# Eighty of 128 expert blocks of U: transposed by VectorE ahead of time and read back from DRAM

## The chip, the cores and the metric

The program runs on one core of a Trainium2 chip. The metric is the device time of one execution in microseconds (us), taken as the median of three executions; lower is better. A separate execution was recorded by the hardware profiler, and every duration in this document is from such a recording.

## The reference, cut to what matters

Two blocks act on 256 tokens of 2048 float32 features. The first is a gated convolution mixer with an MLP (matrices `w_in`, `w_out`, `w_up`, `w_down`). The second is attention (`w_in_2`, `w_uq_2`, `w_ukv_2`, `w_a_proj_2`, `w_b_proj_2`, `w_o_2`) and then an expert layer:

```
q = (h @ w_q)                      # w_peer_q_2
s = q . keys                       # 8 heads, two halves, 128 keys each
expert, gate = best 16 of 16x16 sums per head, softmax   # 128 experts per token
a = einsum('cd,ced->ce', x, u[expert])        # u: 16384 x 2048
w = gelu(a) * gate
y = einsum('ce,ced->cd', w, v[expert])
```

The kernel does not gather 128 rows of u for each token over all 2048 columns. It multiplies the tokens with all 16384 rows of u over columns 640 to 2047, and picks from that product; only columns 0 to 639 are gathered.

## The kernel before, in words

Every matrix product is done in three passes of float32r matmuls: each float32 operand is split into a high part (`hi`, `uh`, written by ScalarE) and the rest (`lo`, `ul`, written by VectorE); TensorE then does hi*hi, hi*lo and lo*hi. `split` (L208, L210) is that pair.

**Dense layers.** `linear` (L268) walks over groups of 512 output columns; for each it walks over chunks of four 128-row blocks of the weight. `load_chunk` loads a chunk of 1 MB with one DMA on SP's queue into `raw` (three buffers), splits it in two halves (`hi` and `lo`, four buffers each) and 24 matmuls of 512 columns follow. After each chunk `bg.pump(pump)` issues queued background work. `post_norm` is the same for `w_out` and `w_down`, with two column groups at once and a normalisation at the end, which writes the next layer's transposed operand `xh`, `xl` through `put_xT`. The last 11 of the operand's 16 row blocks live in `xbh`, `xbl`. In order of time: `w_in`, `w_out`, `w_up`, `w_down`, front of `w_in_2`, `w_uq_2`, `w_ukv_2`, gates of `w_in_2`, projections, `w_o_2`, `w_peer_q_2`.

**U stage** (L1184 to L1230). The 16384 rows are 128 blocks of 128. For a block, one DMA on SP's queue brings 128 x 1408 numbers (704 KB) into `uraw`, two buffers. TensorE transposes it in 11 pieces of 128 x 128 (L1203, issued early by a raised priority), ScalarE and VectorE split the pieces out of PSUM in three units (4, 4 and 3 pieces; `uh`, `ul`, four buffers), and 33 matmuls of 256 columns (L1213 to L1215) form the block's product with all tokens. After a pair of blocks ScalarE copies the result to `L`. Background items (the routing: top 16 and so on, mostly VectorE) are pumped once per unit. Once they are used up, each block is followed by two or three gathered dot products: an indirect DMA from GpSimd's queue (`gt`, 320 KB) and one VectorE instruction (L1174).

**V stage.** The same in the other direction, not touched by the change.

Each engine runs its own queue in order; the order in the queues is the order of the program, modified by a planner that works with expected durations. A tile pool that is closed gives its memory to pools opened later, and their first writes wait for the last use of what lay there.

Of the kernel before, what the change touches and what calls it, by code (L numbers as in the profile page):

```python
# [12 lines left out]
F32 = mybir.dt.float32  # L13
# [7 lines left out]
P = 128  # L21
T = 256
# [10 lines left out]
DU = D - GU  # L33
DN = D - GV


# [16 lines left out]
def tile_conv_mlp_then_attention_peer(ctx, tc, a, out):  # L53
    nc = tc.nc
    PSUM = bass.MemoryType.PSUM

    cp = ctx.enter_context(tc.tile_pool(name="cp", bufs=1))
    sm = ctx.enter_context(tc.tile_pool(name="sm", bufs=3))
# [179 lines left out]
    bg = Background()  # L238

    def load_natural(w):  # L240
# [27 lines left out]
    def linear(load, xs, groups, evac, chunks, pair=1, pump=0, prep=None, skew=False, first=None):  # L268
        last = len(chunks) - 1
        for g0 in range(0, len(groups), pair):  # L270
# [17 lines left out]
            for ci, (k0, nk) in enumerate(chunks):  # L288
                if prep is not None:
                    prep(k0, nk)  # L290
                for g in gs:
# [4 lines left out]
                    else:  # L296
                        for h in range(0, nk, 2):
                            for tt in range(NT):
                                o = accs[g][tt][:, :groups[g][1]]
                                for n in (h, h + 1):  # L300
# [6 lines left out]
                                    nc.tensor.matmul(o, lhsT=xl_, rhs=hi, start=False, stop=s1)  # L307
                    bg.pump(pump)
            for tt in range(NT):
                for ci, g, parts in tail:  # L310
                    mm(ci, g, parts, tt)
                for g in gs:
                    evac(g, tt, accs[g][tt][:, :groups[g][1]])
# [14 lines left out]

    def post_norm(w, xs, gain_ap, chunks, pool, next_gain, prep=None):
        og = pool.tile([P, NT, D // 2], F32, name="og")  # L330
# [4 lines left out]
        def evac(g, tt, acc):  # L335
# [9 lines left out]
            nc.vector.tensor_tensor(scaled[tt, g], acc, gbs[g], ALU.mult)  # L345
            if g == 3:
                ssq = sm.tile([P, 1], F32, name="pn_ssq", tag="ssq")
                nc.vector.tensor_reduce(ssq, sq[tt], AX.X, ALU.add)
                y, _ = rms_scale(ssq, D, f"pn{tt}")
                for c in range(4):  # L350
                    cs = slice(c * W, (c + 1) * W)
                    nc.vector.scalar_tensor_tensor(
                        res[:, tt, cs], scaled[tt, c], y, res[:, tt, cs], ALU.mult, ALU.add
                    )
                    put_xT(tt, list(range(4 * c, 4 * c + 4)), next_gain)
# [65 lines left out]
    with ExitStack() as pa:  # L421
# [139 lines left out]

        with tc.tile_pool(name="pn", bufs=1) as pn:
            post_norm(
                a["w_out"][0], resident(yh, yl), a["mix_post_gain"][0],
                [(0, 4), (8, 4), (12, 4), (4, 4)], pn, "mlp_pre",
            )


    with ExitStack() as pb:
# [3 lines left out]
        with ExitStack() as pup:  # L573
            ev = pup.enter_context(tc.tile_pool(name="ev", bufs=2))
            _, rsq = residual_scales("n1")

            def evac_up(g, tt, acc):
# [9 lines left out]
                chunks_of(KD),  # L587
            )
        with tc.tile_pool(name="pn", bufs=1) as pn:
            zs = {}  # L590

            def prep(k0, nk):
# [6 lines left out]
            def zget(k, tt):  # L599
# [5 lines left out]
                a["w_down"][0], zget, a["mlp_post_gain"][0], chunks_of(DFF // P), pn, "g_mix",  # L605
                prep=prep,
            )


    dr = ctx.enter_context(tc.tile_pool(name="dr", bufs=1, space=bass.MemoryType.DRAM))  # L610
    NEG = -1e30
    BIG = 1e33
    with ExitStack() as pc:
# [4 lines left out]
        with ExitStack() as pat:  # L618
            at = pat.enter_context(tc.tile_pool(name="at", bufs=1))
            xp = pat.enter_context(tc.tile_pool(name="xp", bufs=1))  # L620
            ev = pat.enter_context(tc.tile_pool(name="ev", bufs=2))
            r2, _ = residual_scales("n2", last_xT["g_mix"])
            r2q = []
# [275 lines left out]
            def weave(chains):  # L899
# [10 lines left out]
                [(0, 2)], pump=2,  # L910
            )
            left_ = [swa(*s_) for s_ in spots[4:]]
            late_ = [mla(*s_) for s_ in spots]
# [5 lines left out]
            )  # L919
            bg.flush()  # L920

        with ExitStack() as pj:
            mp = pj.enter_context(tc.tile_pool(name="mx", bufs=1))
            ev = pj.enter_context(tc.tile_pool(name="ev", bufs=2))
# [35 lines left out]
            def evac_o(g, tt, acc):  # L960
# [9 lines left out]
                evac_o, chunks_of(KD), skew=True,  # L970
            )


# [34 lines left out]
    for tt in range(NT):  # L1008
        nc.vector.tensor_tensor(xg[:, tt, :], res[:, tt, 0:GU], gfb, ALU.mult)
        rd = dr.tile([P, D], F32, name=f"res_d{tt}")  # L1010
        nc.scalar.dma_start(rd, res[:, tt, :])
        res_d.append(rd)
    kraw = qp.tile([P, 16, P], F32, name="kraw")
    nc.scalar.dma_start(kraw, a["peer_keys_2"][0].rearrange("h p n d -> n (h p) d"))
# [121 lines left out]
    def load_wq(raw, k0, nk, n0, nw):  # L1136
# [11 lines left out]
        chunks_of(KD), pump=2,  # L1148
    )
    q_ctx.close()  # L1150
    st_ctx.close()
# [37 lines left out]
    for i in range(NE):  # L1189
# [6 lines left out]
        raw = us.tile([P, DU], F32, name="uraw", tag="uraw")  # L1196
        nc.sync.dma_start(raw, a["peer_u_2"][0, i * P:(i + 1) * P, GU:D])
        rawp = raw.rearrange("p (j k) -> p k j", k=KU)
        for k0, nk in UNITS:
            with tc.high_priority(offset=EARLY):  # L1200
                ut = pst.tile([P, 4, P], F32, name="tp_u", tag="tr")
                for kk in range(nk):
                    nc.tensor.transpose(ut[:, kk, :], rawp[:, k0 + kk, :], ident)  # L1203
# [249 lines left out]
```

## Time and profile before

| | us |
|---|---|
| median of three executions | 3265.41 (3259.81 to 3267.61) |
| the profiled execution's own time | 3268.55 |
| span of its trace, first to last instruction | 3266.8 |
| PE (TensorE) busy | 3148.7 (96%) |
| DVE (VectorE) busy | 2213.1 (68%) |
| ACT (ScalarE) busy | 1585.8 (49%) |
| POOL (GpSimd) busy | 852.9 (26%) |
| moved by DMA | 687.06 MB, mean 210 GB/s |

PE and PEld are matmuls and the loads of their stationary operand, which overlap. An engine's busy time counts no waits. The share of the DMA engines is the mean over the core's 16. A mean over the whole span mixes stages with different limits, so the rows below are by stage.

### The profile page before, as it was taken

The numbers are of one execution on the slowest core, as the hardware profiler recorded it, in microseconds if no ns is written. First come the engines' busy times: TensorE is split into PE (matmuls) and PEld (weight loads), VectorE is DVE, ScalarE is ACT, GpSimd is POOL, SyncE is SP. The second block draws the span as 40 slices with busy tenths as digits, with TensorE's granted clock in tenths as the row PEclk, the third lists the DMA queues.
The fourth block names the chain that finished last, engine by engine and source line by source line (L and its number), as shares of the span: only waits on it lengthen the run. The fifth ranks groups of instructions, "written<-read, shape, count | busy, mean of one in ns | idle before, by whom it ended". The sixth has DMA issues, their size and how long they took to land.

```text
span 3266.8 us, 47283 instructions
## 1 busy us (share of the span) xinstructions
PE 3148.7 (96%) x16970; PEld 2659.9 (81%) x16970; DVE 2213.1 (68%) x4331; ACT 1585.8 (49%) x2602; POOL 852.9 (26%) x793
## 2 busy tenths in 40 slices
PE   9899999999999999999999999999999999989998
PEld 7678788887888787777878999999999976667776
DVE  6987644445555655455658877766666977778887
ACT  7555544444454556455454333333333564545554
POOL 1630000000000000000002245544443965555554
PEclk9999999999999999999999999999999999999999
DMA  6445566565555454456664379878886358888887
GB/s 209 131 166 194 165 179 183 178 182 189 193 200 193 143 190 140 161 170 206 207 229 135 125 236 308 308 258 258 258 262 207 125 168 293 278 277 290 288 294 239
DMA packets 284389, 687.06 MB, mean 210 GB/s; under 512 B 23575, under 2 KB 28666, under 8 KB 283898
## 3 DMA queue, kind: packets, MB, share of 16 engines
q1 hardware_dynamic: 234864, 518.58, 47.4%
q0 software_dynamic: 40960, 151.03, 15.1%
q10 hardware_dynamic: 8330, 14.44, 1.3%
q8 instruction: 133, 2.18, 0.3%
q14 instruction: 102, 0.84, 0.1%
HBM read 675.43 MB, written 8.52 MB: 209 GB/s over the span
## 4 chain that ended last, share of the span: by engine, by line
PE 69%; DMA 14%; DVE 9%; issue 4%; POOL 1%; ACT 1%; DVEq 0%; SPq 0%; ACTq 0%; POOLq 0%
PE acc L307 15%; PE acc L306 15%; PE acc L305 15%; DMA gt<-peer_v,e 11%; PE tp_u L1203 5%; PE aps L1215 4%; PE aps L1213 4%; PE aps L1214 4%; DMA uraw<-peer_u 2%; DVE gc L446 2%; DVE lo L210 2%; DVE y L1351 1%; PE ep L1283 1%; PE wp L1314 1%; DVE vl L210 1%
## 5 line engine op out<-in xcount | busy, mean ns | idle before, releaser
L210 DVE TENSOR_TENSOR lo<-raw,hi 128x1024 fp32r<-128x1024 f32 (+2 forms) x580 | 711.7, 1229 | 536.1 <-ACT hi L208 535.5
L208 ACT ACTIVATE hi<-raw 128x1024 fp32r<-128x1024 f32 (+2 forms) x580 | 607.6, 1049 | 584.2 <-PE acc L307 553.4
L1213 PE MATMUL aps<-xbh,uh 128*128 128x256 f32 x1408 | 429.9, 305 | 0.0
L1215 PE MATMUL aps<-xbh,ul 128*128 128x256 f32 x1408 | 425.3, 302 | 0.1
L306 PE MATMUL acc<-lo,xbh 128*128 128x512 f32 (+1 forms) x1034 | 412.9, 400 | 11.8 <-DVE lo L210 11.7
L1214 PE MATMUL aps<-xbl,uh 128*128 128x256 f32 x1408 | 421.5, 299 | 0.0
L307 PE MATMUL acc<-hi,xbl 128*128 128x512 f32 (+1 forms) x1034 | 411.7, 399 | 2.4 <-DVE xbl L212 2.4
L208 ACT ACTIVATE uh<-tp_u 128x512 fp32r<-128x512 f32 (+1 forms) x384 | 215.7, 562 | 398.5 <-PE aps L1214 198.7
L305 PE MATMUL acc<-hi,xbh 128*128 128x512 f32 (+1 forms) x1034 | 408.5, 399 | 0.1
L210 DVE TENSOR_TENSOR ul<-tp_u,uh 128x512 fp32r<-128x512 f32 (+1 forms) x384 | 246.9, 643 | 207.1 <-ACT uh L208 143.3
L1167 POOL DMA_INDIRECT gt<-peer_v,e x256 | 308.2, 1204 | 286.5 <-DVE y L1351 255.4
L208 ACT ACTIVATE vh<-vraw 128x512 fp32r<-128x512 f32 x384 | 239.9, 633 | 284.1 <-DMA vraw<-peer_v 224.4
L1167 POOL DMA_INDIRECT gt<-peer_u,e x256 | 278.0, 1086 | 315.3 <-DVE gt L1174 270.8
L1402 PE MATMUL va<-vl,wh 128*128 128x512 f32 x768 | 315.5, 411 | 41.7 <-DVE vl L210 40.1
L1203 PE MATMUL tp_u<-ident,uraw 128*128 128x128 f32 x1408 | 318.8, 292 | 6.3 <-DMA uraw<-peer_u 4.5
L1403 PE MATMUL va<-vh,wl 128*128 128x512 f32 x768 | 302.2, 394 | 0.0
L1397 PE MATMUL va<-vh,wh 128*128 128x512 f32 x768 | 298.2, 393 | 2.1 <-ACT vh L208 2.0
L1213 PEld LDWEIGHTS aps<-xbh,uh 128*128 128x128 f32 x1408 | 274.8, 195 | 0.0
L1215 PEld LDWEIGHTS aps<-xbh,ul 128*128 128x128 f32 x1408 | 273.8, 194 | 0.3 <-DVE ul L210 0.3
L1214 PEld LDWEIGHTS aps<-xbl,uh 128*128 128x128 f32 x1408 | 273.6, 194 | 0.0
L1351 DVE SCALAR_TENSOR_TENSOR y<-gt,wtok,y 128x512 f32<-128x512 f32 x256 | 191.8, 749 | 113.6 <-DMA gt<-peer_v,e 111.0
L210 DVE TENSOR_TENSOR vl<-vraw,vh 128x512 fp32r<-128x512 f32 x384 | 255.8, 685 | 4.6 <-ACT vh L208 4.6
(534 smaller groups left out, 5974.3 us busy)
## 6 DMA issues: line engine op xcount, KB each, us to landing
vraw<-peer_v SPq DMA_DIRECT2D x384, 256.0 KB
raw<-w_in SPq DMA_DIRECT2D x88, 1024.0 KB
uraw<-peer_u SPq DMA_DIRECT2D x128, 704.0 KB
raw<-w_up SPq DMA_DIRECT2D x64, 1024.0 KB
raw<-w_down SPq DMA_DIRECT2D x64, 1024.0 KB
raw<-w_out SPq DMA_DIRECT2D x16, 1024.0 KB
raw<-w_o SPq DMA_DIRECT2D x16, 1024.0 KB
jb<-jd SPq DMA_DIRECT2D x32, 512.0 KB
```

The source lines that it names most:

```text
L208: op = nc.scalar.activation(hi, src, AF.Copy, scale=scale)
L210: nc.vector.tensor_tensor(lo, src, hi, ALU.subtract)
L305: nc.tensor.matmul(o, lhsT=xh_, rhs=hi, start=s0, stop=False)
L306: nc.tensor.matmul(o, lhsT=xh_, rhs=lo, start=False, stop=False)
L307: nc.tensor.matmul(o, lhsT=xl_, rhs=hi, start=False, stop=s1)
L1167: nc.gpsimd.indirect_dma_start(out=gt, out_offset=None, in_=table, in_offset=bass.IndirectOffsetOnAxis(ap=e4[:, tt, s:s + 1], axis=0),)
L1203: nc.tensor.transpose(ut[:, kk, :], rawp[:, k0 + kk, :], ident)
L1213: nc.tensor.matmul(o, lhsT=uh[:, kk, :], rhs=xbh[:, k, :], start=s0, stop=False)
L1214: nc.tensor.matmul(o, lhsT=uh[:, kk, :], rhs=xbl[:, k, :], start=False, stop=False)
L1215: nc.tensor.matmul(o, lhsT=ul[:, kk, :], rhs=xbh[:, k, :], start=False, stop=s1)
L1402: nc.tensor.matmul(acc[tt][n], lhsT=wh[:, e % 2, tk], rhs=vl, start=False, stop=False)
L1403: nc.tensor.matmul(acc[tt][n], lhsT=wl[:, e % 2, tk], rhs=vh, start=False, stop=s1)
```

## The change

A `Transposer` works on blocks i with i % 8 in (0, 1, 2, 4, 6), 80 of 128, in 160 half blocks of 64 rows. It is pumped after each chunk in `w_out`, `w_up`, `w_down`, the gates, the projections, `w_o` and `w_peer_q`, and at a rate of 0.73 it does one half block at 73 of 100 pumps. One step loads a half block by four DMAs on SP's queue (each 32 partitions by two runs of 352 numbers), transposes the half block loaded one step before with one VectorE instruction of 128 x 704 numbers, and stores that to a DRAM tile `ud` by a DMA from GpSimd's queue. The buffers `tq` and `tu` (two each) lie in pools opened next to the dense layers, and during `w_down` in the memory of `xbh`; there `xbh` is allocated anew near the end (`free_stage`). In the U stage an early block is read back in transposed order, in the same 704 KB, and split straight from `uraw`; its TensorE transposes are left out.

```diff
+QU = DU // 4
+    class Transposer:
+        def __init__(self, blocks):
+            self.todo = [(i, h) for i in blocks for h in range(2)]
+            self.done = {
+                i: dr.tile([P, 2, KU, 64], F32, name=f"ud{i}") for i in blocks
+            }
...
+        def place(self):
+            if self.pool is not None:
+                return (
+                    self.pool.tile([P, 2 * QU], F32, name="tq", tag="tq"),
+                    self.pool.tile([P, 2 * QU], F32, name="tu", tag="tu"),
+                )
+            self.turn = 1 - self.turn
+            o = 4 * QU * self.turn
+            return self.slots[:, o:o + 2 * QU], self.slots[:, o + 2 * QU:o + 4 * QU]
+
+        def pump(self):
+            if self.pool is None and self.slots is None:
+                return
+            self.credit += self.rate
+            if self.credit < 1:
+                return
+            self.credit -= 1
+            before, self.loaded = self.loaded, None
+            if self.todo:
+                i, h = self.todo.pop(0)
+                tq, tu = self.place()
+                for g in range(4):
+                    r, c = i * P + h * 64, GU + g * QU
+                    nc.sync.dma_start(
+                        tq[g * 32:(g + 1) * 32, :].rearrange("p (q c) -> p q c", q=2),
+                        a["peer_u_2"][0, r:r + 64, c:c + QU].rearrange("(q e) c -> e q c", e=32),
+                    )
+                self.loaded = i, h, tq, tu
+            self.finish(before)
+
+        def finish(self, unit):
+            if unit is None:
+                return
+            i, h, tq, tu = unit
+            nc.vector.transpose(
+                tu.rearrange("p (k q e) -> p q k e", q=2, e=32),
+                tq.rearrange("p (q c k) -> p q k c", q=2, k=KU),
+            )
+            nc.gpsimd.dma_start(
+                self.done[i][:, h].rearrange("p k e -> p (k e)"), tu
+            )
+
+        def close(self):
+            self.finish(self.loaded)
+            self.pool = self.slots = self.loaded = None
+
+    pre = Transposer([i for i in range(128) if i % 8 in (0, 1, 2, 4, 6)])
...
                     bg.pump(pump)
+                    pre.pump()
...
             if g == 3:
+                if tt == 0 and before is not None:
+                    before()
...
+            pre.open(0.73, slots=xb_pool.tile([P, 8 * QU], F32, name="stage", tag="xbh"))
+            def free_stage():
+                pre.close()
+                xh.rest = xb_pool.tile([P, KU, T], F32R, name="xbh2", tag="xbh")
...
+            px.close()
+            pre.open(0.73, px.enter_context(tc.tile_pool(name="tp", bufs=2)))
...
         raw = us.tile([P, DU], F32, name="uraw", tag="uraw")
-        nc.sync.dma_start(raw, a["peer_u_2"][0, i * P:(i + 1) * P, GU:D])
-        rawp = raw.rearrange("p (j k) -> p k j", k=KU)
+        early = i in pre.done
+        if early:
+            nc.sync.dma_start(raw, pre.done[i].rearrange("p h k e -> p (h k e)"))
+            rawt = raw.rearrange("p (h k e) -> p k h e", h=2, e=64)
+        else:
+            nc.sync.dma_start(raw, a["peer_u_2"][0, i * P:(i + 1) * P, GU:D])
+            rawp = raw.rearrange("p (j k) -> p k j", k=KU)
         for k0, nk in UNITS:
...
-            split(uh[:, :nk], ul[:, :nk], ut[:, :nk])
+            if early:
+                half = lambda t: t[:, :nk].rearrange("p k (h e) -> p k h e", h=2)
+                split(half(uh), half(ul), rawt[:, k0:k0 + nk])
+            else:
+                with tc.high_priority(offset=EARLY):
+                    ut = pst.tile([P, 4, P], F32, name="tp_u", tag="tr")
+                    for kk in range(nk):
+                        nc.tensor.transpose(ut[:, kk, :], rawp[:, k0 + kk, :], ident)
+                split(uh[:, :nk], ul[:, :nk], ut[:, :nk])
```

## Rows read from the trace of the kernel before

**Rows 1.** Page: busy us by engine; chain that ended last, by engine.

```profile
PE 3148.7 (96%) x16970; PEld 2659.9 (81%) x16970; DVE 2213.1 (68%) x4331; ACT 1585.8 (49%) x2602; POOL 852.9 (26%) x793
PE 69%; DMA 14%; DVE 9%; issue 4%; POOL 1%; ACT 1%; DVEq 0%; SPq 0%; ACTq 0%; POOLq 0%
```

**Rows 2.** Stretches: busy us per engine (instructions), PEclk, DMA share, GB/s.

```profile
365.00:745.00 380.00, 376.72 (x1672) 302.98 (x1671) 193.85 (x235) 187.84 (x249) 0.00 (x0) 0.99 0.58 174
745.00:1105.00 360.00, 357.40 (x1567) 293.15 (x1567) 205.56 (x198) 174.56 (x204) 1.50 (x2) 1.00 0.58 195
1250.00:1490.00 240.00, 236.81 (x1124) 180.37 (x1123) 125.39 (x243) 128.24 (x282) 0.00 (x0) 1.00 0.49 161
1490.00:1675.00 185.00, 185.00 (x832) 151.38 (x831) 107.59 (x117) 92.20 (x114) 0.33 (x2) 1.00 0.63 208
1675.00:1800.00 125.00, 120.40 (x566) 98.34 (x564) 98.19 (x337) 64.43 (x110) 17.35 (x19) 0.97 0.52 176
1800.00:1905.00 105.00, 104.46 (x844) 104.14 (x845) 93.96 (x335) 41.64 (x89) 24.16 (x34) 0.98 0.39 133
1905.00:2130.00 225.00, 220.95 (x1792) 218.49 (x1791) 164.80 (x361) 81.66 (x143) 125.58 (x119) 1.00 0.89 301
2130.00:2500.00 370.00, 367.91 (x3011) 367.72 (x3010) 227.44 (x478) 132.05 (x237) 148.39 (x134) 1.00 0.78 251
```

**Rows 3.** PE's timeline in one U block: start us, us, instruction.

```profile
2258.12 0.29 PE L1203 MATMUL tp_u<-ident,uraw 128*128 128x128 f32 x1
2258.62 0.30 PE L1203 MATMUL tp_u<-ident,uraw 128*128 128x128 f32 x1
2259.00 0.28 PE L1214 MATMUL aps<-xbl,uh 128*128 128x256 f32 x1
2260.19 0.29 PE L1215 MATMUL aps<-xbh,ul 128*128 128x256 f32 x1
```

**Rows 4.** Instruction groups by shape: count, busy us, mean ns, idle before.

```profile
L1203 PE MATMUL tp_u<-ident,uraw 128*128 128x128 f32 x1408 | 318.8, 292 | 6.3 <-DMA uraw<-peer_u 4.5 <-DVE gt L1174 1.4 <-DVE ul L210 0.2
L210 DVE TENSOR_TENSOR ul<-tp_u,uh 128x512 fp32r<-128x512 f32 x256 | 175.8, 687 | 95.9 <-ACT uh L208 52.2 <-PE aps L1215 34.1 <-issue 8.3
L210 DVE TENSOR_TENSOR vl<-vraw,vh 128x512 fp32r<-128x512 f32 x384 | 255.8, 685 | 4.6 <-ACT vh L208 4.6
L210 DVE TENSOR_TENSOR lo<-raw,hi 128x768 fp32r<-128x768 f32 x8 | 7.7, 957 | 10.7 <-ACT hi L208 10.7
L210 DVE TENSOR_TENSOR wl<-L,wh 128x512 fp32r<-128x512 f32 x63 | 67.8, 1076 | 1.2 <-ACT wh L208 1.2
L1275 DVE TENSOR_SCALAR jb<-jb,iota_p 128x1024 f32<-128x1024 f32 x32 | 24.8, 786 | 3.4 <-DMA jb<-jd 3.3
```

**Rows 5.** SP's and ACT's timelines: a w_up chunk issued, then first used.

```profile
503.40 0.37 SPq L242 DMA_DIRECT2D raw<-w_up  x1
...
515.40 1.06 ACT L208 ACTIVATE hi<-raw 128x1024 fp32r<-128x1024 f32 x1 [1.75 <-PE acc L307]
```

**Rows 6.** Stretches, while that chunk's DMA lands and just after.

```profile
504.40:508.60 4.20, 4.20 (x24) 3.50 (x23) 1.72 (x2) 2.14 (x3) 0.00 (x0) 1.00 0.83 250
508.60:509.30 0.70, 0.70 (x4) 0.57 (x3) 0.70 (x1) 0.00 (x0) 0.00 (x0) 1.00 0.00 0
```

**Rows 7.** SP queue's waits in w_up: us, times, longest us.

```profile
SPq L242 <- DVE lo L210: 316.7, 59, 5.8
```

**Rows 8.** Chain of waits, 1905 to 2130 us: by line, one piece.

```profile
by line: DMA uraw<-peer_u 27.4%; PE tp_u L1203 17.2%; PE aps L1215 13.5%; PE aps L1213 13.3%; PE aps L1214 13.1%; issue 12.1%; DVE gt L1174 1.7%; DVE ul L210 1.4%; ACT uh L208 0.8%; SPq L1197 0.5%; DVEq L210 0.0%; ACTq L208 0.0%
1955.15 6.94 DMA uraw<-peer_u
```

**Rows 9.** SP issuing U rows: ns min/median/max, first, last start.

```profile
L1197 SPq DMA_DIRECT2D uraw<-peer_u x128: 327/328/641, 1687.6 to 2483.9; - x128
```

**Rows 10.** Stretches: ten microseconds of dense DMA in the V stage.

```profile
2730.00:2740.00 10.00, 7.73 (x32) 5.48 (x31) 5.51 (x9) 3.61 (x6) 1.84 (x2) 1.00 0.97 359
```

More of the change, by code (lines that the diff above doesn't have):

```diff
@@ L55, in tile_conv_mlp_then_attention_peer @@
     PSUM = bass.MemoryType.PSUM
+    dr = ctx.enter_context(tc.tile_pool(name="dr", bufs=1, space=bass.MemoryType.DRAM))
     cp = ctx.enter_context(tc.tile_pool(name="cp", bufs=1))
@@ L238, in tile_conv_mlp_then_attention_peer, with open @@
     bg = Background()
+    class Transposer:
[5 more added lines that the diff above has]
+            self.pool = self.slots = self.loaded = None
+            self.credit = self.turn = 0
+        def open(self, rate, pool=None, slots=None):
+            self.rate, self.pool, self.slots = rate, pool, slots
+        def place(self):
[39 more added lines that the diff above has]
+            self.finish(self.loaded)
+            self.pool = self.slots = self.loaded = None
+    pre = Transposer([i for i in range(128) if i % 8 in (0, 1, 2, 4, 6)])
     def load_natural(w):
@@ L327, in transposed, with post_norm @@
         return tp
-    def post_norm(w, xs, gain_ap, chunks, pool, next_gain, prep=None):
+    def post_norm(w, xs, gain_ap, chunks, pool, next_gain, prep=None, before=None):
         og = pool.tile([P, NT, D // 2], F32, name="og")
@@ L560, in tile_conv_mlp_then_attention_peer @@
             bg.flush()
-        with tc.tile_pool(name="pn", bufs=1) as pn:
+        with tc.tile_pool(name="pn", bufs=1) as pn, tc.tile_pool(name="tp", bufs=2) as tpool:
+            pre.open(0.73, tpool)
             post_norm(
@@ L574, in tile_conv_mlp_then_attention_peer @@
             ev = pup.enter_context(tc.tile_pool(name="ev", bufs=2))
+            tpool = pup.enter_context(tc.tile_pool(name="tp", bufs=2))
             _, rsq = residual_scales("n1")
+            pre.open(0.73, tpool)
             def evac_up(g, tt, acc):
@@ L588, in tile_conv_mlp_then_attention_peer @@
             )
+            pre.close()
         with tc.tile_pool(name="pn", bufs=1) as pn:
             zs = {}
+            pre.open(0.73, slots=xb_pool.tile([P, 8 * QU], F32, name="stage", tag="xbh"))
+            def free_stage():
+                pre.close()
+                xh.rest = xb_pool.tile([P, KU, T], F32R, name="xbh2", tag="xbh")
             def prep(k0, nk):
@@ L605, in tile_conv_mlp_then_attention_peer @@
                 a["w_down"][0], zget, a["mlp_post_gain"][0], chunks_of(DFF // P), pn, "g_mix",
-                prep=prep,
+                prep=prep, before=free_stage,
             )
-    dr = ctx.enter_context(tc.tile_pool(name="dr", bufs=1, space=bass.MemoryType.DRAM))
+            xbh = xh.rest
     NEG = -1e30
@@ L619, in tile_conv_mlp_then_attention_peer @@
             at = pat.enter_context(tc.tile_pool(name="at", bufs=1))
-            xp = pat.enter_context(tc.tile_pool(name="xp", bufs=1))
             ev = pat.enter_context(tc.tile_pool(name="ev", bufs=2))
+            px = pat.enter_context(ExitStack())
+            xp = px.enter_context(tc.tile_pool(name="xp", bufs=1))
             r2, _ = residual_scales("n2", last_xT["g_mix"])
@@ L920, in tile_conv_mlp_then_attention_peer @@
             bg.flush()
+            pre.close()
         with ExitStack() as pj:
+            pre.open(0.73, pj.enter_context(tc.tile_pool(name="tp", bufs=2)))
             mp = pj.enter_context(tc.tile_pool(name="mx", bufs=1))
@@ L971, in tile_conv_mlp_then_attention_peer @@
             )
+            pre.close()
     NE = 128
@@ L1012, in tile_conv_mlp_then_attention_peer @@
         res_d.append(rd)
+    pre.open(0.73, q_ctx.enter_context(tc.tile_pool(name="tp", bufs=2)))
     kraw = qp.tile([P, 16, P], F32, name="kraw")
@@ L1149, in tile_conv_mlp_then_attention_peer @@
     )
+    pre.close()
+    assert not pre.todo, len(pre.todo)
     q_ctx.close()
@@ L1196, in tile_conv_mlp_then_attention_peer @@
         raw = us.tile([P, DU], F32, name="uraw", tag="uraw")
-        nc.sync.dma_start(raw, a["peer_u_2"][0, i * P:(i + 1) * P, GU:D])
-        rawp = raw.rearrange("p (j k) -> p k j", k=KU)
+        early = i in pre.done
[5 more added lines that the diff above has]
+            rawp = raw.rearrange("p (j k) -> p k j", k=KU)
         for k0, nk in UNITS:
[L1200 to L1203, printed above, removed]
             pool = ring("u")
```

## The prediction

> **What bounds the kernel now.** I read the page first: TensorE is busy for 96% of the span and makes up 69% of the chain that ended last; VectorE is busy for 68% [rows 1]. These are means, so the second view is busy time by stretch [rows 2]. In the dense layers (365 to 1675 us) PE is busy for 98 to 100% of each stretch, VectorE for 51 to 58%, the DMA engines for 49 to 63%: PE sets the pace, and the rest has room. The U stage runs from 1800 to 2500 us and has three parts. In A (1800 to 1905) VectorE is almost as full as PE, 94 of 105 us, since routing is worked off there, and DMA is at 0.39. In B (1905 to 2130) three gathers go with each block: DMA is at 0.89, and the chain of waits in that stretch names the DMA of U rows for 27.4%, with pieces of nearly 7 us [rows 8]. In C (2130 to 2500) there are two gathers per block, DMA is at 0.78, PE at 99%. At 44 PE instructions a block, the counts of rows 2 give 19, 41 and 68 blocks.
>
> **What the change takes off TensorE.** In the timeline of one block [rows 3] a transpose and a matmul alternate between 2258.12 and 2258.62: two pairs in 0.50 us, 0.25 us a pair. From 2259.00 to 2260.19 ten matmuls alone take 1.19 us, 0.119 each. So a transpose costs PE 0.131 us of its time (its shown duration of 292 ns [rows 4] overlaps its neighbours). 80 blocks x 11 = 880 of them go: 115 us of PE. By part, with five of eight blocks early: A 12 x 11 x 0.131 = 17 us, B 25.6 blocks, 37 us, C 42.5 blocks, 61 us.
>
> **What is late next in U.** The DMA brings the same bytes as before, and VectorE's split costs the same from SBUF as from PSUM (685 against 687 ns [rows 4]). So each part gets PE's new time, or what else is in it, if that is longer; as a filled engine I take a share of 0.97, the densest ten microseconds of DMA that I found [rows 10].
> - A: PE 105 - 17 = 88; VectorE 94 / 0.97 = 97. Result 97, a gain of 8.
> - B: PE 225 - 37 = 188; DMA 225 x 0.89 / 0.97 = 206. Result 207, a gain of 18.
> - C: PE 370 - 61 = 309; DMA 370 x 0.78 / 0.97 = 298. The two are within 4%, so neither hides the other's hitches; I take 320, a gain of 50.
>
> Sum 76 us, of the 115 that PE gives up. The bounds are 33 (third rival) and 115 (second).
>
> **VectorE's transposes.** No row shows one. A half block is 128 x 704 numbers. From above: the strided read of L, 128 x 512 in 1076 ns, gives 704 / 512 x 1076 = 1.48 us; from below: a one-operand instruction, 128 x 1024 in 786 ns, gives 0.54; the contiguous split in between, 128 x 768 in 957 ns, gives 0.88 [rows 4]. The transpose reads with a stride, so I take 1.48. 160 of them are 237 us (86 to 237). At 0.73 of 64 pumps, 47 lie in `w_up`: VectorE goes from 194 to 263 of 380 us; in `w_down` from 206 to 275 of 360; in projections and `w_o` (23 of them) from 108 to 142 of 185 [rows 2]. PE's work covers that, for the split runs ahead of PE: ScalarE waits 1.75 us for PE to free `hi` [rows 5]. The cover is thin only in `w_peer_q`: 98 us of 125 plus 12 x 1.48 = 17 makes 92%. I charge 7 there (0 to 17).
>
> **The transfers.** A step moves 0.36 MB in and 0.36 MB out, 115 MB in all. `w_up` moves 174 GB/s at a share of 0.58, so 300 GB/s when full: 2.4 us a step, 113 us, and the share goes from 0.58 to 0.88; in the same way `w_down` goes to 0.86 and projections with `w_o` to 0.90 [rows 2]. B has run at 0.89, so this fits, without much room. The stores wait on GpSimd's queue, which is idle from `w_up` to `w_o` (0 to 1.5 us busy [rows 2]); in `w_peer_q` they stand among its routing items, inside the 7.
>
> **The new wait on SP's queue.** The load of step n goes into the buffer that the transpose of step n-2 has to read first; that transpose stands in VectorE's queue one pump earlier, behind a chunk's splits. SP works in order, so the load of the next weight chunk stands behind this wait, where it used to wait only for `lo` of the chunk three before (316.7 us of such waits in `w_up` [rows 7]: SP is far ahead). A chunk issued at 503.40 had landed by 508.60 and was first used at 515.40 [rows 5, 6]: 6.8 us of slack. A chunk of `w_up` is 26 PE instructions at 380 / 1672 us, 5.9 us, and in `w_down` 24 at 360 / 1567, 5.5 us [rows 2]. Now a load is issued up to a chunk (5.9 us) and a transpose (1.5) later, behind four issues of 0.33 [rows 9] and the step's data (about 1.1): 9.8 us, 3 more than the slack. That lands in the second reserve, the two chunks that `hi` and `lo` hold (11.8 us less half a chunk and 2.3 of splitting, 1.06 on ScalarE and by size 1.28 on VectorE [rows 4, 5]: 6.5 us). The round from split to transpose, load, weight load and split is 1.5 + 1.3 + 1.1 + 5.2 + 3.4 (twice 1.06, once 1.28) = 12.5 us. In eight chunks the chain goes through three rounds and one plain step of 2.5 (27 of 100 pumps do nothing): 40 us, against 8 x 5.5 = 44 at PE's pace. Hidden, then, but the first rival starts here.
>
> The Trainium skill has a rule against these loads ("SBUF — State Buffer", section "Door 1: The DMA port swizzle"): a transfer's rate hangs on how many of 16 ports its partitions reach, and partitions 0 to 31 reach eight, 189 GB/s at 1 MiB. Each of the four loads of a step spans 32 partitions; an estimate by that page is 0.36 MB / 189 GB/s = 1.9 us a step in place of 1.1, a round of 13.3 us, still under PE's pace, and no other sum. No row of this trace shows a large load to 32 partitions.
>
> **Edges.** At each of six openings the first load needs memory whose last user has just finished, and SP's queue holds weight loads behind it. Slack of 6.8 us covers most; I charge 2 us each, 12 (0 to 41). At the end of `w_down` one transpose (1.48) and its store come before `xbh` is written again, behind the norm's small instructions: 2 (0 to 5).
>
> **The sum.** -76 + 7 + 12 + 2 = -55 us. The profiled execution took 3268.55 us, 1.75 over its span; it becomes 3213. It stands 3.1 above the median of the runs, so the forecast is 3210 us.
>
> **Rivals.**
> 1. *Weight loads come late (slower).* Place: SP's queue in the dense layers. The reserve is used up when the round exceeds (44 - 2.5) / 3 = 13.8 us. For it: the round is 12.5 by quiet transfers, and the DMA share nears 0.9. Against: the planner may let weight loads pass a load whose buffer isn't free. At a round of 15.5 us, eight chunks take 49 us: 0.6 us more each over 144 chunks at 5.5 (90 us), 0.2 over the 64 of `w_up` (14): +104 - 55, 3314 us.
> 2. *U follows PE alone.* DMA gives way beyond 0.97 and the gathers fill the gaps: -115 + 21, 3171 us. For it: ten microseconds at 359 GB/s [rows 10] against 301 in B. Against: the chain in B already names the DMA [rows 8].
> 3. *U rows are held too long.* In an early block `uraw` is free only when VectorE's third `ul` is done, behind dot products; before, PE's early transposes freed it. With two buffers and loads of nearly 7 us [rows 8], B gains nothing and C half: -8 - 25 + 21, 3253 us.
>
> **Chances and range.** Forecast 0.52, rival 1 0.18, rival 2 0.17, rival 3 0.13. A difference under 0.3% (10 us) can't be told from none. Forecast, rival 2 and half of rival 3 are faster (0.76), the other half is the same (0.06), rival 1 is slower (0.18). The range is 3160, below rival 2 with its edges cheaper, to 3272, past rival 3; rival 1 is what is left out.
>
> **What would show it.** Right: 528 transposes of `tp_u` are left; PE's pace in early blocks is 33 x 0.119 = 3.9 us; A, B and C take about 97, 207 and 320 us; VectorE's transposes take 0.9 to 1.5 us; the dense stretches keep PE at 97% or more, with a DMA share near 0.87. Wrong: PE waiting for `lo` or `hi` after a late `raw` between 365 and 1675 us (rival 1); a B as long as before (rival 3); a C near 309 and B under 200 (rival 2); a transpose of VectorE far above 1.5 us, which would fill `w_down` and make the splits late without any DMA.

## The result: slower, and the profile after

The changed kernel takes 3320.9 us (median of 4 runs, 3314.7 to 3323.4), the kernel before 3263.9 beside it: ratio 1.0172, interval 1.0152 to 1.0192. The forecast was 3210 us with a range to 3272, so it had the wrong sign. The profiled execution took 3314.74 us, 1.7 over its span. Page of the kernel after, against [rows 1]:

```profile
span 3313.0 us, 47230 instructions
...
PE 3070.0 (93%) x16090; PEld 2558.9 (77%) x16090; DVE 2416.2 (73%) x4491; ACT 1574.1 (48%) x2602; POOL 951.1 (29%) x953
...
PE 38%; DMA 29%; DVE 15%; issue 13%; POOL 3%; SPq 1%; ACT 1%; DVEq 0%; ACTq 0%; POOLq 0%
```

TensorE lost its 880 transposes and is busy for 79 us less, yet the span grew by 46: its share of the last chain fell from 69 to 38%, and DMA's doubled. Where this happened is read by cutting each trace at the first load of each stage (and U at its first matmul, its first gathered dot product and the 117th). One execution each, us (`w_down` with the small projections behind it, `attn` from `w_uq` to the gates; the runs under the first two are explained below):

```
              w_in  w_out   w_up  w_down  attn   proj+w_o  w_peer_q     A      B      C   pick+V, tail
before       264.9   85.8  386.2   472.9  275.2    183.0     135.6   107.9  213.0  375.3     766.9
after        284.1  138.6  384.9   494.6  273.5    197.6     125.6   123.0  200.9  319.7     770.6
dense_alone  285.4  138.0  386.3   493.3  274.6    197.4     138.2   108.4  214.7  371.3     766.5
u_alone      265.7   85.8  385.0   472.7  276.1    183.1     129.1   113.2  207.0  314.8     777.4
pinned       266.3   89.0  424.5   501.7  277.3    194.8     127.5   120.9  204.9  322.9     775.5
lag1_two     266.2   85.8  386.3   476.2  274.3    185.2     130.4   121.2  207.3  319.7     780.7
done_by_wo   266.1   89.3  385.1   478.8  270.0    195.7     126.2   113.8  197.6  320.5     771.1
late_only    265.5   85.8  385.3   479.0  269.2    189.4     128.8   103.9  205.5  315.2     770.5
```

In B and C the changed kernel won 12 and 56 us, about what was forecast (18 and 50). The dense layers took +19, +53, +22 and +15 us (`w_in`, `w_out`, `w_down`, projections with `w_o`), `w_peer_q` -10 and A +15. Stretches of the kernel after (columns as in [rows 2]): `w_in`, `w_out`, `w_up`, `w_down`, projections with `w_o`, then A, B, C:

```profile
10.00:295.00 285.00, 236.43 (x947) 180.00 (x945) 266.27 (x350) 145.68 (x235) 107.71 (x131) 0.95 0.80 257
295.00:433.00 138.00, 109.01 (x453) 87.36 (x454) 96.56 (x111) 56.77 (x65) 9.22 (x17) 0.89 0.70 223
433.00:818.00 385.00, 380.87 (x1699) 306.24 (x1698) 196.42 (x238) 190.00 (x251) 0.00 (x0) 1.00 0.58 175
818.00:1233.00 415.00, 397.11 (x1694) 320.01 (x1693) 289.56 (x315) 193.79 (x258) 27.78 (x52) 0.98 0.79 256
1587.00:1785.00 198.00, 191.30 (x851) 155.39 (x850) 140.56 (x145) 91.48 (x121) 12.46 (x23) 0.98 0.91 290
...
1908.00:2031.00 123.00, 102.49 (x800) 100.31 (x799) 110.19 (x380) 48.38 (x100) 34.56 (x40) 0.92 0.41 137
2031.00:2231.00 200.00, 178.73 (x1407) 172.35 (x1407) 153.23 (x340) 69.02 (x132) 127.48 (x115) 0.99 0.92 325
2231.00:2548.00 317.00, 308.94 (x2530) 305.44 (x2528) 230.95 (x486) 131.45 (x235) 151.72 (x132) 1.00 0.86 293
```

`w_up` is untouched: DMA share 0.58 and no work on POOL, as before. Its 47 steps, and those of `w_out`, were moved ahead of it by the planner, into `w_in` and `w_out` (39 and 19 transposes lie there). The same stages of the kernel before (`w_in`, `w_out`) show what they fell on: in `w_in` VectorE was already at 237 of 265 us (it works the convolution), in `w_out` PE never paused.

```profile
10.00:275.00 265.00, 242.71 (x1017) 190.47 (x1017) 236.97 (x356) 161.47 (x254) 90.67 (x90) 0.97 0.50 166
275.00:361.00 86.00, 86.00 (x381) 70.53 (x380) 48.27 (x48) 40.16 (x46) 0.00 (x0) 1.00 0.62 208
```

At that border SP's queue (start us, us, instructions) is filled with the new loads: 25 in a row, then three weight chunks and none until 354.79.

```profile
283.96 0.38 SPq L306 DMA_DIRECT2D raw<-w_out  x1
284.39 22.84 SPq L279 DMA_DIRECT2D tq<-peer_u  x25
317.52 13.88 SPq L306 DMA_DIRECT2D raw<-w_out  x3
348.06 5.88 SPq L279 DMA_DIRECT2D tq<-peer_u  x8
354.79 0.39 SPq L306 DMA_DIRECT2D raw<-w_out  x1
```

VectorE's timeline at the same border has the transposes, each behind a wait for its own load, ahead of the normalization (`ln_v`) on which `w_out`'s operand depends:

```profile
297.10 1.41 DVE L290 STREAM_TRANSPOSE tu<-tq 128x704 f32<-128x704 f32 x1 [0.50 <-DMA tq<-peer_u]
301.80 1.41 DVE L290 STREAM_TRANSPOSE tu<-tq 128x704 f32<-128x704 f32 x1 [3.28 <-DMA tq<-peer_u]
303.84 1.44 DVE L290 STREAM_TRANSPOSE tu<-tq 128x704 f32<-128x704 f32 x1 [0.64 <-DMA tq<-peer_u]
305.19 0.40 DVE L558 TENSOR_SCALAR ln_v<-va 128x256 f32<-128x256 f32 x1
```

Both forms of the transpose, by shape, and the waits from `w_up` to `w_peer_q` (us, times, longest):

```profile
L290 DVE STREAM_TRANSPOSE tu<-tq 128x704 f32<-128x704 f32 x113 | 167.0, 1478 | 85.5 <-DMA tq<-peer_u 77.5 <-issue 4.9 <-DMA ud<-tu 2.5
...
L290 DVE STREAM_TRANSPOSE stage<-stage 128x704 f32<-128x704 f32 x47 | 69.9, 1488 | 65.8 <-DMA stage<-peer_u 57.2 <-issue 6.8 <-DVE zl L212 0.9
```
```profile
ACT hi L210 <- DMA raw<-w_down: 83.2, 28, 9.3
DVE stage L290 <- DMA stage<-peer_u: 57.2, 29, 4.5
...
DVE tu L290 <- DMA tq<-peer_u: 35.5, 20, 4.3
```

A transpose lasts 1.48 us, as estimated. But VectorE stood still for 135 us at transposes whose load had not landed, and in `w_down` ScalarE waited 83 us for weights. SP's queue was held there too, by loads whose buffer a transpose had yet to read:

```profile
SPq L279 <- DVE stage L290: 100.2, 38, 6.2
```

### The profile page after: what moved, and what is told of

Same layout as the page of the kernel before. It is cut to its first block, busy times and chain, and to the rows that moved or that the text cites. A ratio compares the mean times of both kernels' runs of the same rounds, so it can differ in the third digit from the quotient of the medians.

```text
span 3313.0 us, 47230 instructions
## 1 busy us (share of the span) xinstructions
PE 3070.0 (93%) x16090; PEld 2558.9 (77%) x16090; DVE 2416.2 (73%) x4491; ACT 1574.1 (48%) x2602; POOL 951.1 (29%) x953
## 4 chain that ended last, share of the span: by engine, by line
PE 38%; DMA 29%; DVE 15%; issue 13%; POOL 3%; SPq 1%; ACT 1%; DVEq 0%; ACTq 0%; POOLq 0%
DMA gt<-peer_v,e 12%; PE acc L371 7%; PE acc L370 7%; PE acc L369 7%; DMA tq<-peer_u 4%; DMA stage<-peer_u 4%; PE aps L1310 3%; DVE lo L212 3%; PE aps L1309 3%; PE aps L1308 3%; DVE gc L513 2%; POOL gt L1253 2%; DMA uraw<-peer_u 2%; DVE tu L290 1%; PE ep L1378 1%
## 5 line engine op out<-in xcount | busy, mean ns | idle before, releaser
L212 DVE TENSOR_TENSOR lo<-raw,hi 128x1024 fp32r<-128x1024 f32 (+2 forms) x580 | 703.9, 1221 | 342.5 <-ACT hi L210 342.2
L1310 PE MATMUL aps<-xbh,ul 128*128 128x256 f32 x1408 | 410.1, 291 | 18.4 <-DVE ul L212 18.2
L1308 PE MATMUL aps<-xbh,uh 128*128 128x256 f32 x1408 | 405.4, 288 | 23.3 <-ACT uh L210 23.3
L1309 PE MATMUL aps<-xbl,uh 128*128 128x256 f32 x1408 | 403.4, 287 | 0.0
L1253 POOL DMA_INDIRECT gt<-peer_u,e x256 | 291.3, 1138 | 227.4 <-DVE gt L1260 186.3
L294 POOL DMA_DIRECT2D ud<-tu x113 | 61.7, 546 | 887.4 <-DVE tu L290 593.1
L370 PEld LDWEIGHTS acc<-lo,xbh 128*128 128x128 f32 x1034 | 197.3, 191 | 86.2 <-DVE lo L212 41.3
L1497 PEld LDWEIGHTS va<-vl,wh 128*128 128x128 f32 x768 | 144.9, 189 | 122.2 <-DVE vl L212 94.7
```

The source lines that it names most:

```text
L212: nc.vector.tensor_tensor(lo, src, hi, ALU.subtract)
L370: nc.tensor.matmul(o, lhsT=xh_, rhs=lo, start=False, stop=False)
L1253: nc.gpsimd.indirect_dma_start(out=gt, out_offset=None, in_=table, in_offset=bass.IndirectOffsetOnAxis(ap=e4[:, tt, s:s + 1], axis=0),)
L1308: nc.tensor.matmul(o, lhsT=uh[:, kk, :], rhs=xbh[:, k, :], start=s0, stop=False)
L1309: nc.tensor.matmul(o, lhsT=uh[:, kk, :], rhs=xbl[:, k, :], start=False, stop=False)
L1310: nc.tensor.matmul(o, lhsT=ul[:, kk, :], rhs=xbh[:, k, :], start=False, stop=s1)
```

## The experiments

Theory 1: the dense loss comes from where the planner put the steps. Theory 2: it comes from VectorE's in-order queue, in which a transpose waits for a load issued just before, and the splits behind it come late. Rival A: the added traffic. Rival B: the 237 us that the transposes take of VectorE. Each run was compared with the kernel before on the same chip (3263.6 to 3264.9 us).

**The two halves, and the pin.** `u_alone` does no step and reads plain rows for the early blocks, so that their columns stand in another order:

```
 def pump(self):
-    if self.pool is None and self.slots is None: return
+    return
...
-    nc.sync.dma_start(raw, pre.done[i]...)
+    nc.sync.dma_start(raw, a["peer_u_2"][0, i * P:(i + 1) * P, GU:D])
```


> No half block is loaded ahead, transposed or stored; the 80 early blocks are read from U in its own order and split without being transposed (so their products are of the wrong elements; bytes, instructions and waits of the U stage are those of the changed kernel). If the loss lies in the dense layers alone (theory 1), the time is that of the kernel before less what the U stage gains in the changed kernel, 60 to 65 us: 3200 +- 10. If the U stage gains less than its shorter span suggests, because it only starts with more work already done (rival), it is above 3225.

`dense_alone` does all steps, but U transposes every block on TensorE as before (`early = False`).

> All 160 half blocks are loaded, transposed and stored as in the changed kernel, but no block is read back: the U stage is that of the kernel before, with all its TensorE transposes. Theory 1 (the planner moves the steps of w_out and w_up ahead into w_in, where VectorE is full, and bunches the others): about 105 us above the kernel before, 3370, with 70 of them before the first load of w_up. Rival (the loss is in U or in the reading back): at most 50 above, 3315.

`pinned` holds the four loads of a step behind the weight load of its chunk on SP's queue:

```
+with tc.issue_after(self.anchor.ins):   # anchor: the last raw load
     for g in range(4): nc.sync.dma_start(tq[...], a["peer_u_2"]...)
```


> The changed kernel with one difference: the four loads of a step are issued behind the weight load of the chunk at which the step is written, so that the planner can't move a step ahead of its place. Theory 1: w_in and w_out are as before, steps are spread at 73 of 100 chunks, the dense layers lose 20 to 30 us in all, U gains 60: 3225 to 3240, faster than the kernel before. Rival (the price is of the transfers and transposes wherever they stand, SP's queue and the DMA share among them): 3300 or more, with the loss moved from w_in to w_up.

Measured: `u_alone` 3217.1 us, 0.9857 (0.984 to 0.9873); `dense_alone` 3378.0, 1.0347 (1.033 to 1.0365); `pinned` 3304.2, 1.011 (1.0093 to 1.0127). U gives 48 us, less than the 60 to 65 expected, though more than in its rival; the dense half costs 113, of which 73 lie in `w_in` and `w_out`, as theory 1 had it. `pinned` shows that theory 1 is not enough: `w_in` and `w_out` came back to +1 and +3 us, but `w_up` now lost 38 and `w_down` 29. In `w_up` ScalarE waits only 5.2 us for weights, so they were not late; PE's two longest waits there are for VectorE, for `z` (the layer's results, which PE transposes) and for `lo`. These waits, then VectorE's timeline from 600 us, then SP's:

```profile
PE tp L392 <- DVE z L653: 16.2, 7, 3.1
PE acc L371 <- DVE lo L212: 6.6, 9, 1.4
```

```profile
602.68 1.23 DVE L212 TENSOR_TENSOR lo<-raw,hi 128x1024 fp32r<-128x1024 f32 x1 [0.21 <-ACT hi L210]
610.08 1.50 DVE L291 STREAM_TRANSPOSE tu<-tq 128x704 f32<-128x704 f32 x1 [6.17 <-DMA tq<-peer_u]
611.49 2.34 DVE L212 TENSOR_TENSOR lo<-raw,hi 128x1024 fp32r<-128x1024 f32 x2
614.48 1.49 DVE L291 STREAM_TRANSPOSE tu<-tq 128x704 f32<-128x704 f32 x1 [0.65 <-DMA tq<-peer_u]
615.89 2.32 DVE L212 TENSOR_TENSOR lo<-raw,hi 128x1024 fp32r<-128x1024 f32 x2
622.53 1.44 DVE L291 STREAM_TRANSPOSE tu<-tq 128x704 f32<-128x704 f32 x1 [4.32 <-DMA tq<-peer_u]
```
```profile
601.37 0.39 SPq L307 DMA_DIRECT2D raw<-w_up  x1
601.81 2.02 SPq L280 DMA_DIRECT2D tq<-peer_u  x4
603.94 0.38 SPq L307 DMA_DIRECT2D raw<-w_up  x1
604.37 4.90 SPq L280 DMA_DIRECT2D tq<-peer_u  x4
```

The transpose of 610.08 stands ahead of two `lo` splits and waits 6.17 us. Theory 2 was formed here.

**The lag, and its parts.** `lag` transposes a half block two pumps after its load, behind that pump's last `lo` split, with four load buffers (three in the gates' projections; `xbl`'s dead memory serves in `w_down`, and that stage's `zh`, `zl` pool opens later to make room). `moves_only` keeps this order but stores each half block untransposed; `turns_only` transposes a tile that lies in SBUF all the time, without loads and stores.

```
+self.clock += 1
+while self.flying and self.flying[0][0] <= self.clock - LAG:
+    with tc.issue_after(low[-1].ins):      # low: the lo splits so far
+        self.finish(self.flying.pop(0)[1])
...
-tq bufs=2
+tq bufs=4
```


> As the pinned kernel, but a half block is transposed two pumps after its load, behind that pump's last lo split on VectorE, with four load buffers in place of two; in w_down the dead memory of xbl gives the buffers. Theory 2 (the transpose stands at the head of VectorE's in-order queue and waits for a load issued just before, so that the splits behind it come late): VectorE's wait for tq falls from 285 us to under 40, w_up comes back to 385 to 395 and w_down to 475 to 485, and the total is 3225 to 3245. Rival A (the added traffic slows the weight loads) and rival B (VectorE has no room for 237 us of transposes): w_up stays at 410 or more, the total at 3290 or more.

> As the kernel with the lag, but without the 160 transposes: a half block is loaded and stored again as it is (so the early blocks get untransposed rows), all transfers stay. Theory 2 and rival B: no VectorE queue to block, so the traffic alone costs at most 15 us over the kernel with early blocks and nothing in the dense layers (3217): 3217 to 3232. Rival A: 3275 or more.

> As the kernel with the lag, but without the 640 loads and 160 stores: each of the 160 transposes reads a resident tile behind the same lo split (the early blocks read untransposed rows). Theory 2 and rival A: nothing to wait for, so VectorE's 237 us cost at most 15 us over 3217: 3217 to 3232. Rival B: 3275 or more.

Measured: `lag` 3227.1, 0.9883 (0.986 to 0.9905), faster than the kernel before; `moves_only` 3215.4, 0.9862 (0.9828 to 0.9896); `turns_only` 3217.7, 0.9864 (0.9844 to 0.9884). All transfers without transposes cost nothing over `u_alone`'s 3217, and all transposes without transfers cost nothing either. Rivals A and B fall for these places of the steps, from `w_out` on. `lag` had changed three things against `pinned` (the wait of two pumps, the hold behind a `lo` split, the buffers), so they were parted. `lag1` waits one pump, `lag1_two` one pump with two buffers, `four_bufs` one pump with four buffers and no hold:

```
-LAG = 2                          # lag1, lag1_two, four_bufs
+LAG = 1
-TQ = 4                           # lag1_two
+TQ = 2
-    with tc.issue_after(low[-1].ins):   # four_bufs
```


> As the kernel with the lag, but a half block is transposed one pump after its load instead of two. Theory 2 (a wait in VectorE's in-order queue, which ends as soon as the load has landed): a chunk lasts 5.9 us and a load landed 5.7 us after its issue in the median, so most of the wait is gone, but not the late ones: VectorE waits 20 to 120 us for tq, and the total is 3230 to 3265. If it were the place of the transpose among the splits and not its wait that counts, nothing changes against the lag of two: 3227.

> As the kernel with the lag of one pump (3220.8 us), but the transposes are not held behind a lo split: only the four load buffers (and the memory of xbl in w_down) are left of its difference to the pinned kernel (3304). Theory 2, strictly (VectorE's in-order queue waits at the transpose): buffers alone change little, VectorE waits over 200 us for tq in all, total 3280 or more. Rival (SP's queue: with two buffers the load has to wait for the transpose before it, and so it is issued late): the wait falls to under 80 us, the total to 3220 to 3245.

> As the kernel with the lag of one pump, but with two load buffers as in the changed kernel in place of four. Theory 2, strictly: the place of the transpose alone does it, VectorE waits under 60 us for tq, total 3215 to 3240. Rival (SP's queue holds the load, and the weight loads behind it, until a buffer is free): weight loads come late in w_up and w_down, total 3260 or more.

Measured: `lag1` 3220.8, 0.9855 (0.9836 to 0.9875); `four_bufs` 3306.0, 1.0126 (1.0103 to 1.0149), as slow as `pinned`; `lag1_two` 3232.8, 0.9894 (0.9863 to 0.9924). `four_bufs` and `lag1` differ in the hold alone: the transpose's place is worth 85 us. Buffers give nothing in the order of `pinned` (3304 and 3306); with the hold they give at most 12 us, and the runs of `lag1` and `lag1_two` overlap (3216 to 3226, 3221 to 3241). For `lag1` both the waits forecast, 20 to 120 us, and the total, 3230 to 3265, were too high (7 us, 3220.8); as its waits are gone, this run by itself doesn't part the place from the wait. The loads were no quicker with the hold: the median from issue to landing is 6.8 us in `four_bufs` and 7.3 in `lag1`. VectorE's transposes in `pinned`, `four_bufs` and `lag1_two` (idle time before them last), 113 of the 160; the 47 of `w_down` waited another 125, 126 and 2 us:

```profile
L291 DVE STREAM_TRANSPOSE tu<-tq 128x704 f32<-128x704 f32 x113 | 167.0, 1478 | 285.5 <-DMA tq<-peer_u 285.3
```
```profile
L296 DVE STREAM_TRANSPOSE tu<-tq 128x704 f32<-128x704 f32 x113 | 167.2, 1480 | 295.7 <-DMA tq<-peer_u 287.3 <-DMA ud<-tu 8.2
```
```profile
L297 DVE STREAM_TRANSPOSE tu<-tq 128x704 f32<-128x704 f32 x113 | 167.5, 1483 | 7.0 <-DMA tq<-peer_u 5.7 <-DMA ud<-tu 1.3
```

And `w_up` in `pinned` and in `lag1_two`: the same work, PE busy for 93 and for 99% of it, at a DMA share of 0.83 and 0.87.

```profile
355.00:780.00 425.00, 394.65 (x1704) 312.86 (x1704) 253.30 (x285) 189.87 (x250) 25.47 (x47) 0.97 0.83 241
```
```profile
352.00:737.00 385.00, 380.97 (x1690) 306.20 (x1689) 257.96 (x281) 187.68 (x246) 25.35 (x47) 1.00 0.87 261
```

**The shape of the load.** `two_loads` is `pinned` with two loads over 128 partitions for the four over 32; `two_tall` lets each take 352 columns of all 128 rows, so that its outermost dimension counts 128, not 4.

```
+for q in range(2):     # two_loads; rows r to r + 31
+    nc.sync.dma_start(tq[:, q * QU:(q + 1) * QU], ...[0, r:r + 32, GU:D].rearrange("e (g c) -> g e c", g=4))
+for q in range(2):     # two_tall
+    nc.sync.dma_start(tq[:, q * QU:(q + 1) * QU], ...[0, i * P:(i + 1) * P, c:c + QU])
```


> As the pinned kernel (no lag), but a half block is loaded by two DMAs over 128 partitions each in place of four over 32; the same packets of 1408 bytes in the same places. If the narrow loads are what is slow (the port rule), issue to landing falls from 5.7 us to 3 or less, VectorE's wait for tq to under 100 us, and the total to 3240 to 3260. If it is the queue of weight packets ahead of them and not their shape, landing stays at 5 us or more, the wait above 200 us, and the total at 3290 to 3305.

> As the kernel with two loads over 128 partitions (3610 us), but each load takes 352 columns of all 128 rows, so that its outermost dimension counts 128 and not 4 (these are the wrong elements; packets of 1408 bytes and bytes as before). If a load is spread over DMA engines along its outermost dimension, the packets of a half block now run on far more than 3.3 engines at a time, VectorE's wait for tq falls from 526+216 us to under 350, and the total is 3240 to 3300. If two issues or 128 partitions are what is slow: 3550 or more.

Measured: `two_loads` 3610.5, 1.1061 (1.1041 to 1.1081); `two_tall` 3234.5, 0.9888 (0.9867 to 0.9909). Both totals expected for `two_loads` were wrong. VectorE's waits in them (in `w_down` another 216 and 102 us):

```profile
L291 DVE STREAM_TRANSPOSE tu<-tq 128x704 f32<-128x704 f32 x113 | 164.5, 1456 | 525.8 <-DMA tq<-peer_u 525.8
```
```profile
L290 DVE STREAM_TRANSPOSE tu<-tq 128x704 f32<-128x704 f32 x113 | 167.7, 1484 | 182.2 <-DMA tq<-peer_u 178.1 <-DMA ud<-tu 3.9
```

In `two_loads` 3.3 packets of 1408 bytes were under way at a time (500 to 800 us, mean while any was; at most 7), the 256 of a half block began over about 5.2 us (median). `two_tall` had 6.5 under way, over about 2.3 us; `pinned` 7.5, over about 3 us. The Trainium skill ("DMA: Bandwidth & Descriptors", "Rules for kernel authors") says that the count of the outermost dimension sets how many engines a copy uses, at most four for a count of four: two DMAs with at most 7 packets at once agree. That `two_tall`, with no lag, is 70 us faster than `pinned` supports theory 2 from its other end: its transposes stand at the same place in the program, and VectorE waits 280 us at them in place of 411. It also shows that short waits are covered: in `w_up`, 103 us of them (38 waits) cost 5 us in `two_tall`, 163 us (42 waits) cost 38 in `pinned`. Whether its two issues or its shape made the waits shorter is not parted.

**In the convolution.** `early_lag` is `lag` with steps from `w_in` on.

```
+pre.deep = 3                    # load buffers
+pre.open(0.73, pin.enter_context(tc.tile_pool(name="tp", bufs=2)))   # among w_in's pools
```


> As the kernel with the lag, but the steps begin in w_in, among the convolution on VectorE, where the changed kernel's order put 58 of them (here at 0.73 a chunk, with three load buffers): w_in and w_out took 355 us in the kernel before, 423 in the changed one. If only waits for loads cost time (theory 2), w_in and w_out take 355 to 372 us and the total is 3225 to 3245. If VectorE is simply full there (50 of 50 us in the convolution's stretches), they take 385 or more, the total 3255 or more.

Measured: 3258.0, 0.997 (0.9952 to 0.9987). `w_in` took 279.5 us and `w_out` 127.1, with 10 us of waits for the steps' loads in the whole kernel. So the second expectation came true, and the wait is not all: 15 us go in `w_in`, where VectorE is full for 100 us on end, as in the kernel before, and 41 in `w_out`, where SP's queue has 55 loads of steps in a row and one weight chunk comes 30 us late. In this place theory 1 holds. SP's timeline there, and ScalarE's waits for `w_out` (us, times, longest):

```profile
310.76 34.26 SPq L289 DMA_DIRECT2D tq<-peer_u  x55
```
```profile
ACT hi L214 <- DMA raw<-w_out: 36.7, 3, 30.2
```

**Part A.** `late_only` has no early block below 20; `done_by_wo` keeps all 80, at a rate of 0.8, so that no step is left for `w_peer_q`; `late_more` has 81 of the blocks from 20 on, with steps in `w_peer_q` again.

```
-if i % 8 in (0, 1, 2, 4, 6)
+if i >= 20 and i % 8 in (0, 1, 2, 4, 6)     # late_only
+if i >= 20 and i % 4 < 3                    # late_more
-pre.open(0.73, ...)
+pre.open(0.8, ...)                          # done_by_wo
```


> As the kernel with the lag, but blocks 0 to 19 are not early: 67 early blocks in place of 80, 134 half blocks. If part A of U is set by routing's last items on VectorE, for which the memory of the last buffers waits, then the 13 early blocks there gained nothing (A was 125 us with them, 108 before): A comes to 108 to 116, the dense layers lose one sixth less, and the total is 3205 to 3226. If A follows PE as the prediction had it, their transposes come back: A longer than 125, the total 3230 to 3245.

> As the kernel with the lag (two pumps, 3227 us), but a rate of 0.8 in place of 0.73, so that all 160 half blocks are done in w_o and none stands among the routing in w_peer_q. If VectorE's routing sets w_peer_q and part A together, and a transpose there pushes it on (w_peer_q and A: 256 us with the lag and its 12 transposes, 242 with none of the dense work), they come to 238 to 246 and the total to 3210 to 3218. If the early blocks in A are what delays it, they stay at 250 or more and the total at 3224 or more.

> As the kernel without early blocks below 20 (67 early blocks, 3201.5 us), but with three of four blocks from 20 on early, 81 in place of 67, and 162 half blocks. If PE alone sets part C (316 us with PE busy for 312 and DMA at 0.86), 8.5 blocks more at 1.44 us of PE each make it 12 us shorter: U 611 to 615, the dense layers 2 to 4 us longer, total 3190 to 3196. If C is shared with the DMA engines (its traffic of 377 x 0.78 takes 303 us at a share of 0.97), C stays at 310 or more and B at 205: U 619 or more, total 3199 to 3206.

Measured: `late_only` 3201.5 (3198.4 to 3205.1), 0.9799 (0.9782 to 0.9816), the best of all and below its forecast of 3205; `done_by_wo` 3216.1, as expected, 0.9851 (0.9834 to 0.9869); `late_more` 3225.5, 0.9876 (0.9859 to 0.9892). `w_peer_q` and A together took 244 us before, 242 in `u_alone`, 256 in `lag`, 240 in `done_by_wo`, 233 in `late_only`, 256 in `late_more`. The transposes in `w_peer_q` are none in `u_alone`, `done_by_wo` and `late_only`, 12 in `lag` and 14 in `late_more`: where they stand among the routing, routing ends later, whether A has early blocks or not. What it holds up, in the kernel after: stretches, and waits in the last of them; then the same wait of PE in `u_alone`.

```profile
1995.00:2010.00 15.00, 10.37 (x84) 9.97 (x83) 13.94 (x44) 5.84 (x13) 4.24 (x6) 1.00 0.41 144
2010.00:2025.00 15.00, 3.58 (x16) 3.49 (x17) 11.31 (x40) 1.95 (x6) 5.87 (x8) 0.50 0.14 42
```
```profile
PE aps L1308 <- ACT uh L210: 15.0, 1, 15.0
ACT uh L210 <- DVE e L1187: 7.3, 1, 7.3
```
```profile
PE aps L1306 <- ACT uh L210: 10.8, 1, 10.8
```

By the code, some buffers of `uh` come from the pool `more` from here on, which takes over routing's memory; ScalarE waits there for a late item of routing (`e`). PE stands for 15 us. It stands for 10.8 us in `u_alone` and `done_by_wo`, which have early blocks in A and no transpose in `w_peer_q`, for 19.5 in `lag`, which has both, and not at all in `late_only`: with early blocks PE gets there sooner, and with transposes in `w_peer_q` routing gets there later. `late_more` missed its totals mainly there: with those transposes `w_peer_q` and A took 23 us more than in `late_only`. Its C came to 311.8 us, 3 under `late_only`, where PE alone would have given 12. The DMA of U rows makes up 36% of the chain of waits in C there, 15% in `late_only`, so C is shared with the DMA engines (share 0.88).

## Why the prediction was wrong, step by step

- *PE's gain, B and C*: right. 528 transposes are left; B 201 us (207 forecast), C 320 (320), with DMA at 0.92 and 0.86. `late_more` supports that DMA is the next limit in C, as the two close terms had it. The U sum of 76 was too large all the same: `u_alone`, which has U's part and nothing else, won 48. By its stages `w_peer_q` with A gave 1 for the 8 of A, B and C 6 and 60 for 18 and 50, and pick and V got 10 longer, which no term had.
- *VectorE's transpose*: 1.48 us taken, 1.48 measured. That the stride sets it was not tested; the strided row had the right size.
- *Cover in the dense layers*: the step that failed. The text took "PE's work covers that" from mean shares and charged the dense layers 21 us in all (7, 12 and 2); `dense_alone` measured 113. `turns_only` and `moves_only` show that each part is covered by itself. Together, from `w_up` on, they are not: a transpose that waits for its load keeps the splits behind it waiting too, shown by `four_bufs` against `lag1` (85 us) in the order of `pinned`. In the changed kernel itself this bears on the 22 and 15 us lost in `w_down` and in the projections with `w_o`; the larger loss is the next point. The prediction named SP as the engine that a new wait would block, and put the transpose's own wait for its load at 1.1 us inside a round of 12.5; [rows 5] and [rows 6] were read for the weights' slack only. What stands behind the waiting instruction on VectorE (`lo` and `z`, on which PE depends) was the list to make.
- *Place of the steps*: 47 steps were forecast in `w_up`; none was there. That the planner may move loads was weighed as a point against rival 1, not as a cost. `w_in` and `w_out`, priced at 2 us for one opening, lost 72 us. The place is shown as the cause by `pinned`, which gives back all but 4 of them, and `early_lag` lost 56 there with 10 us of waits for loads in the whole kernel. VectorE's 36 us of such waits in the changed kernel's `w_in` and `w_out` can thus be a part of the 72 only.
- *Rival 1* came out near the time (3314), but by luck: `w_up`, where it put 14 us, lost none, and 19 us were lost in `w_in`, where it put none. Its mechanism is there in part: weights came late at `w_out`'s start and in `w_down`, where SP was held for 100 us and ScalarE waited 83. The same stage has 57 us of VectorE's waits for loads, and in the chain that ended last there the steps' loads are 30%, `w_down`'s 8%; how the 22 us divide is open. In `pinned` SP is held by a step's buffer for only 2 us in `w_down`, and 29 us are lost there all the same.
- *A*: 97 forecast, 123 measured; the 7 us were charged to `w_peer_q`, which in fact ended 10 us sooner. The two together took 249 us, 5 more than before, where a gain of 1 was forecast. VectorE had 94 of 105 us to do in A [rows 2], but what counts is when routing ends: even `u_alone`, with no transpose at all, gained only 1 us over both, since PE stood for 10.8 us at A's end. The 9 transposes that the changed kernel has in `w_peer_q` came on top.
- *Narrow loads*: the 256 packets of a half block began over about 3 us in four loads of 32 partitions (`pinned`), over about 2.3 us in two of 128 (`two_tall`). The Trainium skill's rule on ports ("SBUF — State Buffer", "Door 1: The DMA port swizzle") is not refuted by this and not shown either, since the number of issues changed with it.

The Trainium skill has a rule that VectorE's order in `pinned` goes against ("DMA: Bandwidth & Descriptors", "Rules for kernel authors"): issue the transfer early, compute, and wait for it late. `four_bufs` against `lag1` is that rule by itself here: 3306 and 3221 us.

Left open: how much of the changed kernel's own loss in `w_down` and the projections is VectorE's wait and how much SP's, why pick and V take up to 14 us longer in some kernels with early blocks, why `late_only` needs 11 us less than the kernel before for `w_peer_q` and A, and how the 72 us of `w_in` and `w_out` divide between a full VectorE and SP's queue (`early_lag` shows both, 15 and 41).

## What to carry to other kernels

Before work is put "beside" a stage, list what stands behind its waiting instruction on each in-order queue: in `pinned` a 1.5 us instruction with 6.2 us of wait ahead of it held everything queued behind for 7.7, however idle the engine is by its share. Load one step, use it one step later, and hold the use to its place; the planner here put it right behind its load. And see first whether the stage that gets faster is waiting for something else's end, as A was for routing.

## What the hardware showed beyond that

- Packets of the same size and number (256 of 1408 bytes a half block), in two DMAs with an outermost count of 4 against 128, changed the kernel from 3610 to 3234 us.
- VectorE's transpose of 128 x 704 fp32 with a strided source takes 1.46 to 1.49 us in the mean of every kernel here.
- In the 15 us in which PE had 3.6 us of work, the granted clock was 0.50 (1.2 of 2.4 GHz), against 1.00 in the 15 us before.
